# Every third weight piece splits off its low part by an accumulating GpSimd DMA instead of a VectorE subtraction

## The chip, the cores and the metric

The kernel runs on one core of one Trainium2 chip. The time is the device time of one execution in microseconds (us). Two runs of the kernel before took 2231.20 and 2231.25 us; the median shown is 2231.22 us. One further execution was profiled; its rows are the ones quoted below.

## The reference

The reference is a two-layer encoder trunk on 256 tokens of width 2048 in float32. Layer 0 mixes by neighbourhood attention and a gated recurrence, layer 1 by a pooling mixer and grouped-query attention; each mixer sits between a wide input projection and an output projection, and each layer ends in a SwiGLU with 5632 hidden columns:

```python
for layer in range(DEPTH):                      # DEPTH = 2
    y = ab_mixer(x, ...) if layer % 2 == 0 else cd_mixer(x, ...)
    x = layer_norm(DN_ALPHA * x + y, ln_mix_g[layer], ln_mix_b[layer])
    f = (silu(x @ w_gate[layer]) * (x @ w_up[layer])) @ w_down[layer]
    x = layer_norm(DN_ALPHA * x + f, ln_ffn_g[layer], ln_ffn_b[layer])
```

What matters here are the matrix products `x @ w`: all weights are float32 and each is read once.

## The kernel before, in words

**Tiling.** Each weight matrix is cut into 760 pieces of 512 KB: 128 partitions by two blocks of 512 columns. A chunk of output is 512 columns wide for all 256 tokens (two halves of 128, `tok` 0 and 1), accumulated in PSUM (`acc`) over 8 pieces as a rule. TensorE multiplies in the type fp32r, and to keep float32 accuracy both factors are split into a high part (the value rounded to fp32r) and a low part (what is left): `mm3` (L243) issues three matmuls, high by low, high by high and low by high, so a piece costs 2 blocks x 2 token halves x 3 = 12 matmuls.

**A piece's way** (`load_half`, L127 to L148). SyncE issues the load into `raw`, one of 4 buffers (L140). `split` then makes the parts: ScalarE copies `raw` to `whi`, which rounds (L103), and VectorE subtracts, `wlo = raw - whi` (L104). When the subtraction has ended, the `raw` buffer is free for a later load. `whi` and `wlo` lie in a ring of slots (6 from the pool `wp`, 8 in the second mixer, 11 in the out projections and the SwiGLU, since `open_ring` adds 2 and 3), and a slot is free when TensorE has read the piece that lay there. 128 pieces belong to the input projection of layer 0, 40 to that of layer 1, and 592 to the out projections (32 each) and the SwiGLUs (264 each).

**Order.** A scheduler orders the instructions of each engine ahead of time; every engine then runs its own list in order, and SyncE issues its DMAs in order. `tc.high_priority` draws loads and splits forward as far as the buffers allow.

**Norms.** The last chunk before a layer norm is done token half by token half (`tok_major` in `mm_chunk`), with its 8 pieces held. For each half the norm is: statistics and `centre` on VectorE, the power -0.5 of the variance on GpSimd (`rstd`, L200), the scaling on ScalarE (L288), then `flip`: transposes on TensorE (L100), and `xTh` on ScalarE (L317) and `xTl` on VectorE (L319), while GpSimd adds the bias to the residual (`res`, L320), four instructions for a half. The first chunk after the norm is again token-major: it multiplies half 0 while half 1 is still normed. GpSimd also adds the column mask to the attention bias (L635) and fills two tiles per head pair in the mixer of layer 0 (L520, L521). It issues no DMA.

Of the kernel before, what the change touches and what calls it, by code (L numbers as in the profile page):

```python
# [11 lines left out]
F32 = mybir.dt.float32  # L12
F32R = mybir.dt.float32r
I32 = mybir.dt.int32
AF = mybir.ActivationFunctionType
# [57 lines left out]
def trunk(ctx: ExitStack, tc: tile.TileContext, a, out):  # L73
    nc = tc.nc
    mult, add, sub = ALU.mult, ALU.add, ALU.subtract
# [26 lines left out]
    def split(hi, lo, src):  # L102
        nc.scalar.copy(hi, src)  # L103
        nc.vector.tensor_tensor(lo, src, hi.bitcast(F32), op=sub)  # L104
# [16 lines left out]
    last_load = [None]  # L121
    first = [True]

    def load_half(src, between=()):
        behind = ahead if held[0] > 0 else ()
        held[0] -= 1
        slots = [r for r in rings for _ in range(r[1])]  # L127
        pool, bufs = rings[0] if turn[0] < 0 else slots[turn[0] * 3 % len(slots) if len(slots) % 3 else turn[0] % len(slots)]
        turn[0] += 1
        with tc.high_priority(offset=400):  # L130
            raw = wp.tile([P, 2, NCH], F32, tag="raw", name="raw", bufs=4)
            hi = pool.tile([P, 2, NCH], F32R, tag="whi", name="whi", bufs=bufs)
            lo = pool.tile([P, 2, NCH], F32R, tag="wlo", name="wlo", bufs=bufs)
            parts = 1 + len(between)
            n = 2 // parts
            for i in range(parts):
                if i:
                    between[i - 1]()
                s = slice(i * n, (i + 1) * n)
                load = nc.sync.dma_start(raw[:, s, :], src[:, s, :])  # L140
                if first[0]:
                    tc.keep_in_program_order(load)
                last_load[0] = load.ins
                with ExitStack() as order:
                    for ins in behind:
                        order.enter_context(tc.issue_after(ins))
                    split(hi[:, s, :], lo[:, s, :], raw[:, s, :])
        return hi, lo  # L148

    def mm_chunk(halves, lhs, outs, tok_major=False, after=None, before=None):  # L150
# [17 lines left out]
        if tok_major:  # L168
            for i, (src, _) in enumerate(halves):
                if pending and i >= FREE:  # L170
                    held[0] = 1
                loaded.append(load_half(src))
            for tok in range(NT):
                for i in range(n):
                    if pending and i >= FIRST_STEP:
                        step()
                    mms(i, tok, True)
                    if pending and tok == 0:
                        held[0] = HELD
                while pending:  # L180
                    step()
                if after:
                    after(tok)
        else:
            for i, (src, _) in enumerate(halves):
                loaded.append(load_half(src, before(i) if before else ()))
                for tok in range(NT):
                    mms(i, tok)
            if after:
                for tok in range(NT):  # L190
                    after(tok)
# [721 lines left out]
def build(nc, arrays):  # L913
    args = {}
    for name, v in arrays.items():
        t = nc.dram_tensor(name, v.shape, mybir.dt.from_np(v.dtype), kind="ExternalInput")
        args[name[3:]] = t.ap()
    out = nc.dram_tensor("out", (T, D), F32, kind="ExternalOutput").ap()
    with tile.TileContext(nc, schedule_with_timeline_sim=True) as tc:
        trunk(tc, args, out)  # L920
# [11 lines left out]
```

## Time and profile before

| what | value |
|---|---|
| median of the runs | 2231.22 us |
| the profiled execution's own time | 2229.76 us |
| its span, first to last instruction | 2228.0 us |
| mean granted TensorE clock | 0.996 |
| TensorE busy | 2201.6 us (99%) |
| VectorE busy | 1313.6 us (59%) |
| ScalarE busy | 994.5 us (45%) |
| GpSimd busy | 83.1 us (4%) |
| DMA, mean over the span | 189 GB/s |

The profiled execution took 1.76 us more than its span, and 1.46 us less than the median of the runs. Busy times of TensorE are unions of overlapping matmuls. In the rows, PE is TensorE's matmul, PEld its weight load, DVE VectorE, ACT ScalarE, POOL GpSimd, SP SyncE. A row of instructions has start, duration, engine, line, operation, output and inputs; what stands in brackets is the engine's idle time before it and who ended that.

### The profile page before, as it was taken

The numbers are of one execution on the slowest core, as the hardware profiler recorded it, in microseconds if no ns is written. First come the engines' busy times: TensorE is split into PE (matmuls) and PEld (weight loads), VectorE is DVE, ScalarE is ACT, GpSimd is POOL, SyncE is SP. The second block draws the span as 40 slices with busy tenths as digits, with TensorE's granted clock in tenths as the row PEclk, the third lists the DMA queues.
The fourth block names the chain that finished last, engine by engine and source line by source line (L and its number), as shares of the span: only waits on it lengthen the run. The fifth ranks groups of instructions, "written<-read, shape, count | busy, mean of one in ns | idle before, by whom it ended". The sixth has DMA issues, their size and how long they took to land.

```text
span 2228.0 us, 26810 instructions
## 1 busy us (share of the span) xinstructions
PE 2201.6 (99%) x10180; PEld 1833.9 (82%) x10180; DVE 1313.6 (59%) x1662; ACT 994.5 (45%) x1258; POOL 83.1 (4%) x67
## 2 busy tenths in 40 slices
PE   8999999999999999999999999999999999999997
PEld 7888888887888888888888788878888888888886
DVE  6886688667555545554455676665554554544454
ACT  6445544546443444344443564444444444444431
POOL 0010001002000000000000200020000000000001
PEclk9999999999999999999999999999999999999999
DMA  8555545676655556565656464656555555656562
GB/s 293 161 161 180 173 130 183 219 250 211 205 187 191 190 188 194 184 199 184 197 176 199 151 207 141 235 171 227 188 190 192 186 192 186 198 179 201 183 197 71
DMA packets 118898, 420.66 MB, mean 189 GB/s; under 512 B 14448, under 2 KB 17008, under 8 KB 117488
## 3 DMA queue, kind: packets, MB, share of 16 engines
q1 hardware_dynamic: 118768, 418.94, 57.4%
q8 instruction: 80, 1.31, 0.2%
q14 instruction: 50, 0.41, 0.1%
HBM read 416.78 MB, written 2.10 MB: 188 GB/s over the span
## 4 chain that ended last, share of the span: by engine, by line
PE 96%; DVE 2%; ACT 1%; DMA 0%; issue 0%; POOL 0%; DVEq 0%; ACTq 0%; POOLq 0%
PE acc L243 91%; PE tr L100 2%; PE mx L530 1%; PE mx L243 1%; DVE wlo L104 1%; DVE xTl L319 0%; PE mx L576 0%; PE mx L783 0%; ACT whi L103 0%; ACT res L288 0%; DVE res L274 0%; DMA raw<-in_cd_in 0%; DMA x<-in_xT 0%; DVE res L278 0%; PE mx L766 0%
## 5 line engine op out<-in xcount | busy, mean ns | idle before, releaser
L104 DVE TENSOR_TENSOR wlo<-raw,whi 128x1024 fp32r<-128x1024 f32 (+1 forms) x761 | 938.4, 1236 | 726.2 <-ACT whi L103 708.8
L103 ACT CAST whi<-raw 128x1024 fp32r<-128x1024 f32 (+1 forms) x761 | 800.6, 1053 | 987.4 <-PE acc L243 836.2
L243 PE MATMUL acc<-whi,xTl 128*128 128x512 f32 x2080 | 814.7, 394 | 13.7 <-DVE xTl L319 8.0
L243 PE MATMUL acc<-whi,xTh 128*128 128x512 f32 x2080 | 814.4, 392 | 0.0
L243 PE MATMUL acc<-wlo,xTh 128*128 128x512 f32 x2080 | 808.7, 391 | 0.3 <-DVE wlo L104 0.3
L243 PEld LDWEIGHTS acc<-whi,xTl 128*128 128x128 f32 x2080 | 392.3, 189 | 93.5 <-DVE xTl L319 8.5
L243 PEld LDWEIGHTS acc<-wlo,xTh 128*128 128x128 f32 x2080 | 392.0, 188 | 81.6 <-DVE wlo L104 0.7
L243 PEld LDWEIGHTS acc<-whi,xTh 128*128 128x128 f32 x2080 | 392.4, 189 | 78.5
L243 PE MATMUL acc<-whi,yTl 128*128 128x512 f32 x960 | 375.0, 391 | 0.1
L243 PE MATMUL acc<-whi,yTh 128*128 128x512 f32 x960 | 373.8, 389 | 0.0
L243 PE MATMUL acc<-wlo,yTh 128*128 128x512 f32 x960 | 370.0, 389 | 0.0
L243 PEld LDWEIGHTS acc<-wlo,yTh 128*128 128x128 f32 x960 | 180.2, 188 | 37.8 <-DVE wlo L104 0.4
L243 PEld LDWEIGHTS acc<-whi,yTl 128*128 128x128 f32 x960 | 180.3, 188 | 37.0 <-DVE yTl L789 0.3
L243 PEld LDWEIGHTS acc<-whi,yTh 128*128 128x128 f32 x960 | 180.3, 188 | 36.7
L200 POOL TENSOR_TENSOR rstd<-rstd,mhalf 128x4 f32<-128x4 f32 (+2 forms) x18 | 17.6, 976 | 1799.8 <-DVE rstd L197 1656.9
L104 DVE TENSOR_TENSOR yTl<-tr,yTh 128x512 fp32r<-128x512 f32 x48 | 31.1, 686 | 79.5 <-ACT yTh L103 79.5
L103 ACT CAST yTh<-tr 128x512 fp32r<-128x512 f32 x48 | 26.0, 589 | 94.4 <-PE tr L100 94.3
L320 POOL TENSOR_TENSOR res<-res,bet 128x512 f32<-128x512 f32 x24 | 39.4, 1650 | 26.0 <-PE tr L100 14.6
L259 DVE TENSOR_TENSOR res<-res,acc 128x512 f32<-128x512 f32 x32 | 21.9, 685 | 25.4 <-PE acc L243 24.9
L530 PEld LDWEIGHTS mx<-qq,kk 128*128 128x128 f32 x256 | 33.6, 191 | 2.6
L530 PE MATMUL mx<-qq,kk 128*128 128x128 f32 x256 | 33.8, 274 | 0.0
L257 DVE SCALAR_TENSOR_TENSOR res<-res,acc 128x512 f32<-128x512 f32 x32 | 21.8, 683 | 16.7 <-PE acc L243 15.7
(162 smaller groups left out, 829.4 us busy)
## 6 DMA issues: line engine op xcount, KB each, us to landing
raw<-in_gate SPq DMA_DIRECT2D x176, 512.0 KB, 3.9
raw<-in_up SPq DMA_DIRECT2D x176, 512.0 KB, 4.3
raw<-in_down SPq DMA_DIRECT2D x176, 512.0 KB, 4.1
raw<-in_ab_in SPq DMA_DIRECT2D x127, 512.0 KB, 4.1
raw<-in_cd_in SPq DMA_DIRECT2D x40, 512.0 KB, 4.3
raw<-in_ab_out SPq DMA_DIRECT2D x32, 512.0 KB, 4.7
raw<-in_cd_out SPq DMA_DIRECT2D x32, 512.0 KB, 4.0
x<-in_xT SPq DMA_DIRECT2D x8, 256.0 KB, 6.3
```

The costliest lines, as they stand in the source:

```text
L100: return nc.tensor.transpose(o, src, eye)
L103: nc.scalar.copy(hi, src)
L104: nc.vector.tensor_tensor(lo, src, hi.bitcast(F32), op=sub)
L200: nc.gpsimd.tensor_tensor(r[:, :n], r[:, :n], mhalf[:, :n], op=ALU.pow)
L243: ins = nc.tensor.matmul(o, lhs[a], rhs[b], start=start and n == 0, stop=stop and n == 2)
L257: nc.vector.scalar_tensor_tensor(r, r, ALPHA, psum, op0=mult, op1=add)
L259: nc.vector.tensor_tensor(r, r, psum, op=add)
L320: nc.gpsimd.tensor_tensor(r, r, bet[:, s], op=add)
L530: nc.tensor.matmul(m[:, 2 * h + s, :], kk[:, h, s * P : (s + 1) * P], qq[:, h, r * P : (r + 1) * P], start=True, stop=True,)
```

## The change

Of the 760 pieces every third one (those with a `between`, the first, apart) is split by `split_by_dma`: 253 pieces. ScalarE copies `raw` to `whi` as before, then writes `wlo = -whi` with a second instruction, and a DMA issued on GpSimd's queue adds `raw` to `wlo` in SBUF. The sum is left as a float32 word and isn't rounded to fp32r. VectorE does nothing for these pieces. The diff:

```diff
@@ -121,7 +121,17 @@
     last_load = [None]
     first = [True]
 
+
+    pieces_in = [0]
+
+    def split_by_dma(hi, lo, raw):
+        nc.scalar.copy(hi, raw)
+        nc.scalar.activation(lo, hi.bitcast(F32), AF.Copy, scale=-1.0)
+        nc.gpsimd.dma_start(lo.bitcast(F32), raw, accum_op=add)
+
     def load_half(src, between=()):
+        pieces_in[0] += 1
+        by_dma = pieces_in[0] % 3 == 0 and not between
         behind = ahead if held[0] > 0 else ()
         held[0] -= 1
         slots = [r for r in rings for _ in range(r[1])]
@@ -144,7 +154,7 @@
                 with ExitStack() as order:
                     for ins in behind:
                         order.enter_context(tc.issue_after(ins))
-                    split(hi[:, s, :], lo[:, s, :], raw[:, s, :])
+                    (split_by_dma if by_dma else split)(hi[:, s, :], lo[:, s, :], raw[:, s, :])
         return hi, lo
```

In the changed kernel all lines behind the insertion stand 10 further down: L140 becomes L150, L320 becomes L330, and so on; the copy, the negation and the DMA of a third piece have the lines L128, L129 and L130. The lists of the engines move with it, at two places that the prediction speaks of.

The first is SyncE's list in the first down projection of layer 0. In brackets is what an instruction waits for: a name with DMAHW is a load, DVE is VectorE, a name with DMASW one of eight semaphores that the adds of GpSimd's queue use in turn. Before:

```order
L140 DMA raw_5558<-in_down0 128x1024 [waits DMAHW4_49,DVE_49]
L140 DMA raw_5576<-in_down0 128x1024 [waits DMAHW5_49,DVE_49]
L140 DMA raw_5594<-in_down0 128x1024 [waits DMAHW6_49,DVE_49]
L140 DMA raw_5616<-in_down0 128x1024 [waits DMAHW7_49,DVE_49]
L140 DMA raw_5634<-in_down0 128x1024 [waits DMAHW0_49,DVE_49]
L140 DMA raw_5652<-in_down0 128x1024 [waits DMAHW1_49,DVE_49]
```

Every load waited for a subtraction. Now the same place reads (raw_5591, raw_5646 and raw_5705 are third pieces):

```order
L150 DMA raw_5610<-in_down0 128x1024 [waits DMAHW4_49,DVE_49]
L150 DMA raw_5628<-in_down0 128x1024 [waits DMAHW3_49,DMASW4_49]
L150 DMA raw_5646<-in_down0 128x1024 [waits DMAHW5_49,DVE_49]
L150 DMA raw_5665<-in_down0 128x1024 [waits DMAHW7_49,DVE_49]
L150 DMA raw_5687<-in_down0 128x1024 [waits DMAHW6_49,DMASW5_49]
L150 DMA raw_5705<-in_down0 128x1024 [waits DMAHW0_49,DVE_49]
L150 DMA raw_5724<-in_down0 128x1024 [waits DMAHW2_49,DVE_49]
L150 DMA raw_5742<-in_down0 128x1024 [waits DMAHW1_49,DMASW6_49]
```

One load in three now waits for an add, and it is that of the third piece five pieces earlier: raw_5687 waits for the add of raw_5591, with raw_5610, raw_5628, raw_5646 and raw_5665 between. The load right behind the waiting one is a third piece's own.

The second place is GpSimd's list at the norm between the out projection and the SwiGLU of layer 0. Before (res0 and res1 are the residuals of token halves 0 and 1):

```order
L200 TENSOR_TENSOR rstd_4366<-rstd_4366,mhalf_70 128x1 [waits DVE_49]
L320 TENSOR_TENSOR res0_3792<-res0_3792,bet_3803 128x512 [waits DMAHW2_49,DMAHW5_49,PE_49,Activation_49]
L320 TENSOR_TENSOR res0_3792<-res0_3792,bet_3803 128x512 [waits PE_49,Activation_49] x3
L200 TENSOR_TENSOR rstd_4485<-rstd_4485,mhalf_70 128x1 [waits DVE_49]
L320 TENSOR_TENSOR res1_3793<-res1_3793,bet_3803 128x512 [waits DMAHW3_49,PE_49,Activation_49]
L320 TENSOR_TENSOR res1_3793<-res1_3793,bet_3803 128x512 [waits PE_49,Activation_49] x3
```

Now (wlo_4567, wlo_4586 and wlo_4605 belong to pieces 2, 5 and 8 of the first gate chunk, wlo_4808 to the up chunk behind it):

```order
L130 DMA wlo_4567<-raw_4565 128x1024 [waits DMASW5_49,DMAHW3_49,DVE_49,Activation_49]
L210 TENSOR_TENSOR rstd_4419<-rstd_4419,mhalf_70 128x1 [waits DVE_49]
L130 DMA wlo_4586<-raw_4584 128x1024 [waits DMAHW6_49,DMASW6_49,Activation_49]
L330 TENSOR_TENSOR res0_3834<-res0_3834,bet_3845 128x512 [waits PE_49] x2
L330 TENSOR_TENSOR res0_3834<-res0_3834,bet_3845 128x512 [waits PE_49,Activation_49] x2
L210 TENSOR_TENSOR rstd_4538<-rstd_4538,mhalf_70 128x1 [waits DVE_49]
L330 TENSOR_TENSOR res1_3835<-res1_3835,bet_3845 128x512 [waits PE_49,Activation_49] x3
L130 DMA wlo_4605<-raw_4603 128x1024 [waits DMAHW1_49,DMASW7_49,Activation_49]
L130 DMA wlo_4808<-raw_4806 128x1024 [waits DMAHW4_49,DMASW0_49,Activation_49]
L330 TENSOR_TENSOR res1_3835<-res1_3835,bet_3845 128x512 [waits PE_49]
```

The add of the last piece of the gate chunk stands behind three of the four residual additions of half 1. At the two other norms that a token-major chunk follows, the list has the same pattern: the add of that chunk's eighth piece behind three additions to the residual of half 1.

## The prediction

> **What bounds the kernel now.** I read the page first, then the stretches by stage, the chain of waits in one of them, and the waits.
>
> ```profile
> span 2228.0 us, 26810 instructions
> PE 2201.6 (99%) x10180; PEld 1833.9 (82%) x10180; DVE 1313.6 (59%) x1662; ACT 994.5 (45%) x1258; POOL 83.1 (4%) x67
> q1 hardware_dynamic: 118768, 418.94, 57.4%
> ...
> PE 96%; DVE 2%; ACT 1%; DMA 0%; issue 0%; POOL 0%; DVEq 0%; ACTq 0%; POOLq 0%
> ```
>
> TensorE is busy for all but 26.4 us of the span, and 96% of the chain that ended last is its own work. VectorE, which the change relieves, is 2% of that chain. The stretches say where the 26.4 us lie (columns: stretch, its length, busy us of PE, PEld, DVE, ACT, POOL with counts, clock, DMA share, GB/s):
>
> ```profile
> 0.00:60.00 60.00, 54.34 (x235) 44.43 (x236) 38.19 (x52) 36.51 (x47) 1.67 (x9) 1.00 0.80 281
> 60.00:440.00 380.00, 380.00 (x1956) 323.27 (x1955) 287.04 (x530) 180.54 (x274) 24.80 (x18) 1.00 0.55 169
> 520.00:1160.00 640.00, 636.00 (x2846) 527.11 (x2845) 332.27 (x309) 274.74 (x294) 6.49 (x4) 1.00 0.59 195
> 1500.00:2140.00 640.00, 640.00 (x2865) 530.71 (x2864) 326.61 (x298) 271.09 (x278) 0.00 (x0) 1.00 0.59 193
> ```
>
> In the SwiGLUs and in the first mixer TensorE never waits; it does so only at the start, at the norms and at the end. The chain in a SwiGLU gives the pace:
>
> ```profile
> 1581.97 43.57 PE acc L243 x192
> 1625.54 0.88 PE tr L100 x8
> 1626.41 13.62 PE acc L243 x60
> ```
>
> 192 matmuls, 16 pieces, take 1626.41 - 1581.97 = 44.44 us with the transposes: 2.78 us per piece. And the waits show who waits for whom in steady work:
>
> ```profile
> ACT whi L103 <- PE acc L243: 836.2, 590, 11.2
> ...
> PE acc L243 <- DVE wlo L104: 0.3, 1, 0.3
> ```
> ```profile
> SPq L140 <- DVE wlo L104: 1587.2, 684, 13.1
> ```
>
> ScalarE's copies wait for slots that TensorE has not left yet, so the split parts lie ready far ahead; TensorE waits 0.3 us in all directly for a low part. SyncE waits for subtractions, since these free the `raw` buffers. There is little to win: even with no idle moment the matmuls need 2201.6 us of span, 1.2% less.
>
> **The change part by part.** The split's own instructions:
>
> ```profile
> L104 DVE TENSOR_TENSOR wlo<-raw,whi 128x1024 fp32r<-128x1024 f32 x759 | 937.0, 1238 | 725.8 <-ACT whi L103 708.5 <-PE acc L243 0.4
> L103 ACT CAST whi<-raw 128x1024 fp32r<-128x1024 f32 x759 | 799.3, 1054 | 987.0 <-PE acc L243 836.2 <-issue 65.8 <-DMA raw<-in_ab_out 17.7
> ```
>
> *Removed*: 253 x 1.238 = 313 us of VectorE. They lie beside TensorE's work nearly everywhere, so I count nothing for them; the gain is a rival. *Added on ScalarE*: 253 negations of the copy's size, 253 x 1.054 = 267 us; ScalarE comes to 1261 us, 57%, and its idle time in front of the copies alone is 987 us, so this is hidden while a slot is the last to come. *Added on GpSimd*: 253 adds. The trace has no DMA from GpSimd and none with arithmetic, so I bound one add, from its issue to its landing, by the nearest rows (L140 between 1500 and 2140 us; a store from SBUF; POOL's shortest and longest groups):
>
> ```profile
> DMA to landing us min/median/max: 3.3/4.2/6.1
> ```
> ```profile
> out<-res SPq DMA_DIRECT2D x8, 256.0 KB, 2.3
> ```
> ```profile
> L200 POOL TENSOR_TENSOR rstd<-rstd,mhalf 128x4 f32<-128x4 f32 (+2 forms) x18 | 17.6, 976 | 1799.8 <-DVE rstd L197 1656.9
> L635 POOL TENSOR_TENSOR bias<-bias,colmask 128x512 f32<-128x512 f32 x8 | 17.6, 2206 | 97.2 <-ACT pth L103 55.3 <-DMA bias<-in_na_bias 39.2 <-ACT whi L103 2.7
> ```
>
> A piece occupies the DMA engines for 57.4% x 2228 us / 418.94 MB x 0.524 MB = 1.6 us. From below, the add is the 2.3 us of a store of half the size plus half a piece: 3.1 us. From above it is the slowest load, 6.1 us, two further passes over the data, 3.2 us, and 2.2 us of GpSimd: 11.5 us. I take a load's median of 4.2 us, since the add moves a load's bytes under the same traffic, plus one pass for reading the low part too, 1.6 us, plus 1.0 us for GpSimd to issue it: **6.8 us**.
>
> [...]
>
> *The wait that this moves* is that of SyncE. In the list of the changed kernel the load five pieces behind a third piece waits for its add, and the load behind that one is a third piece's own. So from one third piece to the next but one, six pieces or 6 x 2.78 = 16.7 us, there follow each other: the add, a load's landing 4.2 us, the next load 1.6 us behind it, copy 1.05, negation 1.05, and the next add. The add may last 16.7 - 7.9 = **8.8 us** before the ring of `raw` buffers turns slower than TensorE. At 6.8 us it fits with 2 us to spare, and the 11 slots keep ten pieces of lead. Steady stages: 0.
>
> *The norms* have no such cover. At the first one:
>
> ```profile
> 519.23 1.29 POOL L320 TENSOR_TENSOR res<-res,bet 128x512 f32<-128x512 f32 x1 [3.18 <-ACT res L288]
> 521.05 6.11 POOL L320 TENSOR_TENSOR res<-res,bet 128x512 f32<-128x512 f32 x3 [0.53 <-PE mx L100]
> ...
> 523.04 0.40 PE L243 MATMUL acc<-wlo,xTh 128*128 128x512 f32 x1
> ...
> 528.57 0.50 PE L243 MATMUL acc<-whi,xTl 128*128 128x512 f32 x1 [4.00 <-DVE xTl L319]
> ```
>
> The add of the gate chunk's eighth piece stands behind the third addition, which ended at 521.05 + 2 x 6.11 / 3 = 525.1. Its landing is then at 531.9, where TensorE wanted this low part at 523.04. Behind it come four matmuls (0.9 us) and four transposes (0.44 us), so half 1 begins at 533.3 instead of 528.57: 4.7 us. The other two norms have the same pattern:
>
> ```profile
> 1261.77 1.71 POOL L320 TENSOR_TENSOR res<-res,bet 128x512 f32<-128x512 f32 x1 [0.53 <-PE tr L100]
> ...
> 1264.01 6.15 PE acc L243 x27
> ```
> ```profile
> 1489.24 6.12 POOL L320 TENSOR_TENSOR res<-res,bet 128x512 f32<-128x512 f32 x3 [0.53 <-PE mx L100]
> ...
> 1496.76 3.35 PE acc L243 x7
> ```
>
> 1263.5 + 6.8 + 1.3 = 1271.6 against 1264.0 is 7.6 us; 1493.3 + 6.8 + 1.3 = 1501.4 against 1496.8 is 4.6 us. Together 16.9 us.
>
> *The start* has no lead either. Piece 3 is copied here, and its first low part is wanted here:
>
> ```profile
> 11.71 1.05 ACT L103 CAST whi<-raw 128x1024 fp32r<-128x1024 f32 x1 [0.63 <-DMA raw<-in_ab_in]
> ...
> 14.44 0.39 PE L243 MATMUL acc<-wlo,xTh 128*128 128x512 f32 x1
> ```
>
> Copy and negation end at 13.8, the add lands at 20.6: 6.2 us late.
>
> *The mixers*: with 6 slots a third piece is needed five pieces after its slot came free, 13.9 us later, and is ready after 1.05 + 1.05 + 6.8 = 8.9 us: 5.0 us to spare. An add that stands behind a waiting GpSimd instruction can lose that:
>
> ```profile
> 345.43 1.29 POOL L635 TENSOR_TENSOR bias<-bias,colmask 128x512 f32<-128x512 f32 x1 [20.83 <-DMA bias<-in_na_bias]
> 350.03 7.21 POOL L635 TENSOR_TENSOR bias<-bias,colmask 128x512 f32<-128x512 f32 x1 [3.31 <-DMA bias<-in_na_bias]
> ```
>
> Most waits of this kind end within the spare; the first of these can hold an add for some 10 us, 5 more than there are. I count one: 5 us; none would be 0, all of them is a rival.
>
> **The sum.** On the profiled execution's 2229.76 us: 0 + 16.9 + 6.2 + 5 = 28.1, so 2257.9; the median of the runs lies 1.46 us higher: **2259 us**, 1.2% slower, which is within the 2% that a measurement of this kernel can tell from no change. With an add of 3.1 us the norms cost 5.8, the start 2.5 and the mixers nothing: 2240. This forecast ends where the add passes 8.8 us, with about 2276.
>
> **The rivals.** *The raw ring turns slower than TensorE.* For it: the spare is 2 us in a quantity that I have only by analogy, and loads and adds stretch each other on engines that are 59% busy. Against it: slots ten pieces deep, which smooth single delays. At 10 us per add each six pieces take 1.2 us more; 592 pieces make 592 / 6 x 1.2 = 118, and norms and start 4 x 3.2 = 13 on top: 2390. It decides from 8.8 us on, and passes 2% some 0.1 us later. *The DMA engines are the bound*: if reading, reading and writing pass one after the other, an add takes 4.8 us of them, and three pieces 4.8 + 4.8 = 9.6 instead of 8.33. Over 592 / 3 thirds that is 250 us: 2510. The point is 3.5 us per add. For it speaks that no row shows the arithmetic; against it that a load's 1.6 us holds a read and a write already. *GpSimd's list holds adds in the mixers*: ten waits there, each 3.5 us past the spare, give 35: 2294; for it the 20.83 us row, against it that most such waits in the trace begin long before anything is due. *A gain*: at the norms subtractions are in TensorE's way:
>
> ```profile
> 521.55 6.70 DVE wlo L104 x3
> ...
> 1474.04 3.45 DVE wlo L104 x2
> ...
> 1491.95 4.50 DVE wlo L104 x2
> ```
>
> If these 14.6 us vanished and the add took 3.1 us, the time would be 2231 + 8.4 - 14.6 = 2225. Against it: only one piece in three is relieved.
>
> **How the numbers follow.** Forecast 0.44 (its own range 2238 to 2276), raw ring 0.26 (to 2430), DMA engines 0.16 (to 2700), GpSimd's list 0.08, gain 0.06. Slower by over 2% are the ring, the engines and the list: 0.50. Within 2%: 0.44 and nearly all of the gain, 0.49. Faster by over 2%, under 2187, would need more than the 26.4 us of idle: 0.01. The range leaves out the gain's part below 2236 and the engine case beyond 2500.
>
> **What would show it.** Right: L130 issues on GpSimd land in 6 to 8 us, TensorE stays full between 1500 and 2140 us, and new waits of PE for DMA into `wlo` appear at 14, 523, 1263 and 1490 us. Wrong: in that stretch PE waits for `wlo` regularly and its busy share falls, with SyncE waiting for the adds (raw ring: DMA share under 0.9; engines: near 1); or the waits of PE sum up between 60 and 440 us behind L635, L520 or L200 (GpSimd's list).

## The result, and the profile after

| | before | after |
|---|---|---|
| median of the runs, us | 2231.22 (2 runs) | 2378.35 (2 runs, 2376.8 to 2379.9) |
| profiled execution, us | 2229.76 | 2376.8 |
| its span, us | 2228.0 | 2375.0 |
| mean granted clock of TensorE | 0.996 | 0.977 |

The ratio is 1.0659, 95% interval 1.0614 to 1.0705: the change makes the kernel 147 us slower. The forecast was 2259 us. The figure nearest to the measured one is that of the first rival, the ring of `raw` buffers, 2390 us.

The matmuls, L243 before, are L253 in the changed kernel. The page of the changed kernel, in the same parts as that of before (the last rows are DMA issues: instructions, KB each, median us from issue to landing):

```profile
span 2375.0 us, 27620 instructions
...
PE 2250.5 (95%) x10180; PEld 1854.9 (78%) x10180; DVE 1000.3 (42%) x1409; ACT 1239.8 (52%) x1511; POOL 296.2 (12%) x320
...
q1 hardware_dynamic: 118768, 418.94, 52.9%
q0 software_dynamic: 36432, 132.66, 29.2%
...
DMA 57%; PE 24%; issue 11%; ACT 4%; DVE 2%; SPq 1%; POOL 0%; POOLq 0%; ACTq 0%; DVEq 0%
...
wlo<-raw POOLq DMA_DIRECT2D x253, 512.0 KB, 7.0
raw<-in_gate SPq DMA_DIRECT2D x176, 512.0 KB, 5.4
```

The chain that ended last was 96% TensorE's; now 57% of it is time in which a DMA is under way. The loss divides in two. TensorE's idle time went from 26.4 to 2375.0 - 2250.5 = 124.5 us, 98 more. And the same 10180 matmuls are busy for 2250.5 us where it was 2201.6, 49 more, at a lower granted clock. The stretches (columns as before: length, busy us of PE, PEld, DVE, ACT, POOL, clock, DMA share, GB/s) say where:

```profile
60.00:440.00 380.00, 378.11 (x1942) 320.60 (x1941) 242.33 (x490) 218.61 (x317) 54.15 (x56) 1.00 0.78 222
560.00:1220.00 660.00, 634.52 (x2774) 520.27 (x2773) 218.54 (x211) 334.45 (x346) 66.80 (x76) 0.98 0.86 239
1600.00:2260.00 660.00, 633.33 (x2778) 520.58 (x2777) 219.55 (x211) 335.40 (x347) 66.31 (x76) 0.98 0.86 239
```

The first mixer is nearly full, as forecast. In the SwiGLUs TensorE now idles 26 us in 660, and the DMA engines are at 0.86, under 0.9: of the marks set down for the raw ring these two have come. So has the third, that SyncE waits for the adds:

```profile
SPq L150 <- DMA wlo<-raw: 1056.4, 245, 9.1
SPq L150 <- DVE wlo L104: 616.0, 257, 8.2
```
```profile
ACT whi L103 <- DMA raw<-in_down: 153.4, 80, 6.0
ACT whi L103 <- PE acc L253: 144.4, 96, 5.7
...
ACT whi L128 <- PE acc L253: 84.7, 69, 5.1
```

SyncE's loads wait for 245 of the 253 adds, since these hold the `raw` buffers. ScalarE's copies, which waited 836 us for slots that TensorE had yet to leave, wait 144 us for them and those of the third pieces 85, and otherwise for loads: the slots are no longer full.

The last mark, that TensorE waits for `wlo` regularly, has not come in the SwiGLUs. Between 560 and 1220 us its waits, 25.4 us, all end with the instructions that empty its accumulators: L384, L267 and L269 on VectorE, L377 on ScalarE. The largest part of them, and VectorE just before the longest one (TensorE's idle time there is 4.32 us, and its next instruction starts at 863.62):

```profile
PE tr L100 <- DVE sil L384: 11.0, 3, 4.3
```
```profile
861.75 1.23 DVE L104 TENSOR_TENSOR wlo<-raw,whi 128x1024 fp32r<-128x1024 f32 x1 [3.68 <-ACT whi L103]
862.89 1.28 DVE L384 TENSOR_TENSOR sil<-sil,acc 128x512 f32<-128x512 f32 x2
```

In VectorE's list the product L384 stands behind the subtraction of a piece that was drawn forward. This subtraction waits for ScalarE's copy, and that one stood behind the copy and negation of a third piece whose load landed only at 858.5. So late loads reach TensorE through the order of the lists. The four other waits of over 3 us in this stretch (up to 646.66, 732.90, 1003.43 and 1142.57) have a subtraction with a late copy just before them in the same way.

The chain inside the first SwiGLU shows the ring turning (start, length, what):

```profile
838.60 9.57 DMA wlo<-raw
...
849.11 9.43 DMA raw<-in_up
...
858.61 2.56 issue
...
861.18 4.76 DMA wlo<-raw
...
866.38 4.38 DMA raw<-in_up
...
870.82 3.93 issue
...
874.77 10.31 DMA wlo<-raw
```

An add lands; a load that waited for its buffer goes out, and right behind it a third piece's own load, which is the one shown; that piece is copied and negated (the stretch called issue); its add goes out. No matmul stands in this chain. Two turns, each from a third piece to the next but one, take 874.77 - 838.60 = 36.2 us, 18.1 each, where six pieces take TensorE 16.7. The load's leg is 9.43 in the first turn, where two other loads and an add had gone out within 1 us ahead of it, and 4.38 in the second, where one load had. The times to landing (us, min/median/max), first of the adds and then of the loads, between 560 and 1220 us:

```profile
DMA to landing us min/median/max: 4.4/8.2/10.8
```
```profile
DMA to landing us min/median/max: 3.3/5.2/10.2
```

By stage, counted from the start of the multiplication that makes `rstd` of the second token half at each of the four norms (the small GpSimd instruction on 128x1), in us and with the difference from before:

| kernel | start to norm 1 | norm 1 to 2 (SwiGLU 0) | norm 2 to 3 (mixer, out projection) | norm 3 to 4 (SwiGLU 1) |
|---|---|---|---|---|
| before | 515.05 | 740.47 | 227.80 | 735.46 |
| after | +26.2 | +47.2 | +24.7 | +49.0 |
| swiglu_only | +2.2 | +50.7 | 0.0 | +42.6 |
| swiglu_only_raw6 | +2.0 | -1.7 | 0.0 | -2.6 |
| outside_only | +26.6 | +3.6 | +27.4 | +5.7 |
| mixers_only | +12.0 | 0.0 | +10.7 | 0.0 |
| norms_only | +2.0 | +3.5 | +13.1 | +3.9 |
| out_proj_only | +6.2 | +0.3 | +2.3 | +0.2 |

The first stage of kernels that begin alike spreads by some 2 us. So of 147 us the two stages of the SwiGLUs lost 96, and the rest of the program 51. The late adds behind norms 1 and 3 fall into the stages of the SwiGLUs. The kernels in the lower rows are experiments, told below.

### The profile page after: what moved, and what is told of

Read it like the earlier page. It is cut to its first block, busy times and chain, and to the rows that moved or that the text cites. A ratio compares the mean times of both kernels' runs of the same rounds, so it can differ in the third digit from the quotient of the medians.

```text
span 2375.0 us, 27620 instructions
## 1 busy us (share of the span) xinstructions
PE 2250.5 (95%) x10180; PEld 1854.9 (78%) x10180; DVE 1000.3 (42%) x1409; ACT 1239.8 (52%) x1511; POOL 296.2 (12%) x320
## 3 DMA queue, kind: packets, MB, share of 16 engines
q1 hardware_dynamic: 118768, 418.94, 52.9%
q0 software_dynamic: 36432, 132.66, 29.2%
## 4 chain that ended last, share of the span: by engine, by line
DMA 57%; PE 24%; issue 11%; ACT 4%; DVE 2%; SPq 1%; POOL 0%; POOLq 0%; ACTq 0%; DVEq 0%
DMA wlo<-raw 28%; PE acc L253 20%; DMA raw<-in_down 10%; DMA raw<-in_gate 8%; DMA raw<-in_up 7%; DMA raw<-in_ab_in 2%; DMA raw<-in_cd_in 1%; ACT whi L103 1%; SPq L150 1%; PE mx L540 1%; DVE wlo L104 1%; DMA raw<-in_ab_out 1%; PE mx L253 1%; PE tr L100 1%; ACT whi L128 1%
## 5 line engine op out<-in xcount | busy, mean ns | idle before, releaser
L104 DVE TENSOR_TENSOR wlo<-raw,whi 128x1024 fp32r<-128x1024 f32 (+1 forms) x508 | 623.4, 1232 | 1180.8 <-ACT whi L103 1143.0
L103 ACT CAST whi<-raw 128x1024 fp32r<-128x1024 f32 (+1 forms) x508 | 529.4, 1046 | 660.9 <-DMA raw<-in_down 153.4
L253 PE MATMUL acc<-wlo,xTh 128*128 128x512 f32 x2080 | 817.8, 395 | 35.3 <-DMA wlo<-raw 34.7
L253 PE MATMUL acc<-whi,xTl 128*128 128x512 f32 x2080 | 824.3, 397 | 18.4 <-ACT sil L377 7.7
L253 PE MATMUL acc<-whi,xTh 128*128 128x512 f32 x2080 | 820.5, 394 | 0.0
L253 PEld LDWEIGHTS acc<-wlo,xTh 128*128 128x128 f32 x2080 | 395.8, 190 | 121.3 <-DMA wlo<-raw 38.5
L253 PEld LDWEIGHTS acc<-whi,xTl 128*128 128x128 f32 x2080 | 396.4, 191 | 104.2 <-ACT sil L377 12.0
L253 PEld LDWEIGHTS acc<-whi,xTh 128*128 128x128 f32 x2080 | 396.2, 190 | 79.8
L130 POOL DMA_DIRECT2D wlo<-raw x253 | 221.4, 875 | 1890.8 <-ACT wlo L129 1722.0
L128 ACT CAST whi<-raw 128x1024 fp32r<-128x1024 f32 x253 | 266.1, 1052 | 340.4 <-PE acc L253 84.7
L253 PE MATMUL acc<-whi,yTl 128*128 128x512 f32 x960 | 382.4, 398 | 24.9 <-DVE res L269 13.1
L253 PE MATMUL acc<-wlo,yTh 128*128 128x512 f32 x960 | 376.4, 397 | 10.6 <-DMA wlo<-raw 10.6
L253 PE MATMUL acc<-whi,yTh 128*128 128x512 f32 x960 | 379.2, 395 | 0.0
L129 ACT ACTIVATE wlo<-whi 128x1024 fp32r<-128x1024 f32 x253 | 268.4, 1061 | 7.0
L253 PEld LDWEIGHTS acc<-whi,yTl 128*128 128x128 f32 x960 | 183.9, 192 | 67.0 <-DVE res L269 15.9
L253 PEld LDWEIGHTS acc<-wlo,yTh 128*128 128x128 f32 x960 | 183.4, 191 | 51.7 <-DMA wlo<-raw 12.4
L253 PEld LDWEIGHTS acc<-whi,yTh 128*128 128x128 f32 x960 | 183.7, 191 | 37.8
L100 PE MATMUL tr<-ident,sil 128*128 128x128 f32 x176 | 28.6, 300 | 22.8 <-DVE sil L384 22.8
L100 PEld LDWEIGHTS tr<-ident,sil 128*128 128x128 f32 x176 | 22.9, 153 | 29.8 <-DVE sil L384 26.7
L104 DVE TENSOR_TENSOR yTl<-tr,yTh 128x512 fp32r<-128x512 f32 x48 | 31.4, 685 | 25.4 <-ACT yTh L103 25.0
L330 POOL TENSOR_TENSOR res<-res,bet 128x512 f32<-128x512 f32 x24 | 37.0, 1575 | 31.2 <-PE mx L100 19.2
```

Of the source, the lines that this page charges most:

```text
L100: return nc.tensor.transpose(o, src, eye)
L128: nc.scalar.copy(hi, raw)
L129: nc.scalar.activation(lo, hi.bitcast(F32), AF.Copy, scale=-1.0)
L130: nc.gpsimd.dma_start(lo.bitcast(F32), raw, accum_op=add)
L253: ins = nc.tensor.matmul(o, lhs[a], rhs[b], start=start and n == 0, stop=stop and n == 2)
L330: nc.gpsimd.tensor_tensor(r, r, bet[:, s], op=add)
```

## The experiments

Theory 1 is the raw ring: an add holds a `raw` buffer so long that the four buffers turn slower than TensorE. Theory 2 is that the DMA engines have too much work. Theory 3 is that ScalarE's negations and the order of the engines' lists cost the time. Every ratio is to the kernel before on the same chip, with its 95% interval.

**Ring, engines or lists: four kernels.** *raw6*: two more `raw` buffers in the memory of the out projections and SwiGLUs, the split as in the change.

```diff
-            raw = wp.tile([P, 2, NCH], F32, tag="raw", name="raw", bufs=4)
+            k = raws_in[0] % (4 + more[1])
+            raws_in[0] += 1
+            if k < 4:
+                raw = wp.tile([P, 2, NCH], F32, tag="raw", name="raw", bufs=4)
+            else:
+                raw = more[0].tile([P, 2, NCH], F32, tag="raw", name="raw", bufs=more[1])
...
+        more[:] = [fp, 2]
         xT = out_proj(...)
```

> The changed kernel with six instead of four raw buffers in the out projections and the SwiGLUs; every load there then reuses the buffer of six pieces earlier. Theory 1, the raw ring: an add of 8 us holds a buffer too long for four buffers, so with six the pace returns to 2.78 us per piece there, the DMA share staying near 0.86 to 0.9, and only norms, start and mixers cost: 2265 to 2295 us. Theory 2, the DMA engines: three loads and an add fill them so unevenly that the pace is theirs, whatever the buffers: 2350 to 2380 us. Theory 3, the lists: the second ScalarE instruction and the reordered lists cost the time: 2360 to 2380 us.

*bystander*: the kernel before, and in the out projections and SwiGLUs an adding DMA of the high part of each third piece into scratch memory, whose sum nothing reads.

```diff
                     split(hi[:, s, :], lo[:, s, :], raw[:, s, :])
+                    if scrap and pieces_in[0] % 3 == 0:
+                        nc.gpsimd.dma_start(scrap[pieces_in[0] % 2], hi.bitcast(F32), accum_op=add)
```

> The kernel before, with an accumulating GpSimd DMA of 512 KB for every third piece of the out projections and SwiGLUs that adds the piece's high part to a scratch tile that nothing reads: 197 adds with the engines' full load, but none frees a raw buffer and TensorE waits for none. Theory 1: the engines have room, loads land later but in time: 2231 to 2245 us. Theory 2: the loads starve as in the changed kernel: 2320 to 2360 us. Theory 3 has no say here beyond 2231, since VectorE still splits.

*vector_add*: copy and negation stay on ScalarE, VectorE does the add.

```diff
-        nc.gpsimd.dma_start(lo.bitcast(F32), raw, accum_op=add)
+        nc.vector.tensor_tensor(lo, raw, lo.bitcast(F32), op=add)
```

> The changed kernel with the add of the third pieces on VectorE in place of the DMA (copy and negation on ScalarE, then low part plus raw words on VectorE). Theories 1 and 2: without the DMA the loss is gone, 2228 to 2240 us. Theory 3: the negation on ScalarE and the list around it cost most of the 147 us, so 2300 us or more.

*plain_copy*: the DMA writes the raw words over the low part; the subtraction of those pieces is left out.

```diff
-        nc.gpsimd.dma_start(lo.bitcast(F32), raw, accum_op=add)
+        nc.gpsimd.dma_start(lo.bitcast(F32), raw)
```

> The changed kernel with the GpSimd DMA copying the raw words over the negated high part instead of adding them (the addition is left out, so the low parts of the third pieces are other numbers). Issue, wait and landing stay, and only the second read of the add goes: by half the packet time, 0.16 instead of 0.33 us per 4 KB, a DMA should land some 1.5 to 3 us earlier, at 5 to 6 us. Theory 1: that brings six pieces of the ring to 16.7 us or less, 2255 to 2290 us. Theory 2: the engine time of three pieces falls from 7.4 to 6.2 us, so 2255 to 2290 us as well; the two part here only by whether loads still land late. Theory 3: 2360 to 2380 us.

| kernel | median us | ratio |
|---|---|---|
| raw6 | 2316.8 | 1.0383 [1.0368, 1.0399] |
| bystander | 2251.0 | 1.0086 [1.0069, 1.0103] |
| vector_add | 2232.5 | 1.0002 [0.9993, 1.0011] |
| plain_copy | 2261.1 | 1.0130 [1.0115, 1.0145] |

Theory 3 loses the negations with vector_add: 253 of them, and 253 additions on VectorE in place of the subtractions, cost nothing and gain nothing. The order of the lists with a DMA in them is plain_copy's question, below. Theory 2 loses its strongest form with bystander. Its stretch in the first SwiGLU, and the landing of its own adds there:

```profile
560.00:1160.00 600.00, 599.31 (x2684) 496.44 (x2683) 307.43 (x278) 254.60 (x262) 64.05 (x74) 1.00 0.90 258
```
```profile
scrap<-whi POOLq DMA_DIRECT2D x198, 512.0 KB, 7.2
raw<-in_gate SPq DMA_DIRECT2D x176, 512.0 KB, 6.2
```

The engines carry more than in the changed kernel, 0.90 against 0.86, with as many adds, and TensorE is full. What was taken away is that a `raw` buffer and a low part wait for an add, and the negations, which vector_add acquits. The page also gives the prices at TensorE's own pace: an add 7.2 us, a load 5.8 to 6.2 by weight matrix, where the loads of before took 4.2. Bystander's loss of 19 us, 6 more than the expectation allowed, lies in the stages with the out projections (14.8 and 9.9 us; the stages of the SwiGLUs changed by -4.75 and 0.15); its cause there was not followed.

raw6 is half a success, 22 us above the expected range. In the SwiGLUs its loss is gone (norm 1 to 2: 742.0 us, +1.6; norm 3 to 4: 739.1, +3.7). But the stages with the out projections lost 41.5 and 45.7 us, more than in the change. A wait of SyncE's queue tells why:

```profile
SPq L157 <- DVE yTl L806: 34.3, 1, 34.3
```

The changed kernel has no such wait: the two new buffers lie in memory that the second mixer still used, and the queue goes in order, so one load held up all behind it for 34 us. It is a mishap of this kernel, and swiglu_only_raw6 below is free of it. Why the first of the two stages lost more than in the change is not shown.

plain_copy has as many DMAs of the same size behind the same instructions, and in the stages of the SwiGLUs it loses 0.6 and 2.4 us; so the order of the lists does not by itself cost the 96 us either. Its 29 us lie in the two other stages (11.7 and 17.3). Its DMAs land in 4.3 us at the median, and hold the engines for less:

```profile
q0 software_dynamic: 36432, 132.66, 14.4%
...
wlo<-raw POOLq DMA_DIRECT2D x253, 512.0 KB, 4.3
```

14.4% of a span of 2260.0 us over 253 is 1.29 us of the engines for a copy; in the changed kernel 29.2% of 2375.0 over 253 is 2.74 us for an add. So the arithmetic doubles the transfer, and it is the add's length that the ring does not bear.

**Threshold or price per add, and where: four kernels.** A further theory 4 says that each add costs the same, 147 / 253 = 0.58 us, wherever it stands. A condition chooses the pieces; `part` holds the stage and whether the chunk is token-major:

```diff
-        by_dma = pieces_in[0] % 3 == 0 and not between
+        by_dma = pieces_in[0] % 3 == 0 and not between and (part[0] == "ffn" and not part[1])
```

*swiglu_only* has this line.

> Pieces are split by the DMA add only in the SwiGLUs, without the two token-major chunks of each (about 165 adds of 253); four raw buffers as in the change. Theory 1 (the raw ring, a threshold): the two SwiGLUs lost 47 and about 48 us in the changed kernel, and they lose it here again: 2232 + 95 = 2327. Theory 4 (each add costs the same wherever it stands, 147 / 253 = 0.58 us): 2232 + 165 x 0.58 = 2328. This run alone does not tell the two apart; the next three do.

*swiglu_only_raw6* has it too, and two more buffers, used from the first piece of a SwiGLU on:

```diff
+            k = raws_in[0] % 6 if more[0] else 0
...
+        more[0] = fp
         xT = ffn(fp, 0, xT, res, load_gb(fp, 0, "ffn"), False)
```

> The same pieces as in swiglu_only, and two more raw buffers, taken from the SwiGLU's own memory and used only once the SwiGLU has begun. Theory 1: the ring has room, TensorE is full, 2230 to 2237. Theory 4: as many adds, so 2328 as without the buffers.

*outside_only* has the opposite condition, `part[0] != "ffn" or part[1]`.

> The complement of swiglu_only: the add only in the mixers, the out projections and the token-major chunks at the norms (about 88 adds); four raw buffers. Theory 1: what is left of the loss, 147 - 95 = 52 us: 2284, nearly all of it before the first norm (26) and between the second and the third (25). Theory 4: 2232 + 88 x 0.58 = 2283. If the sum of this loss and of swiglu_only's is far under 147, the parts feed each other.

*sixth_piece*: `pieces_in[0] % 6 == 0` in place of `% 3`, everywhere.

> The add for every sixth piece instead of every third, everywhere (126 adds); four raw buffers. Theory 1: one add in a turn of 12 pieces, 33 us, in which the chain of add, load, load, copy and negation of 16 to 25 us fits with room: the SwiGLUs lose nothing, and what remains is half of the norms and the out projections: 2232 + 10 to 30 = 2242 to 2262. Theory 4: half of the loss, 2232 + 73 = 2305.

| kernel | median us | ratio |
|---|---|---|
| swiglu_only | 2307.6 (2292.4 to 2325.2) | 1.0317 [1.0268, 1.0365] |
| swiglu_only_raw6 | 2225.9 | 0.9971 [0.9960, 0.9982] |
| outside_only | 2293.2 | 1.0277 [1.0261, 1.0293] |
| sixth_piece | 2258.0 | 1.0119 [1.0103, 1.0135] |

Theory 4 falls twice: half as many adds cost 26 us and not 73, and 164 adds in the SwiGLUs cost 76 us with four buffers and less than nothing with six. The losses of swiglu_only and outside_only, 76 and 61, make 137 of 147, so the stages stand nearly for themselves. The expectations had been 2327 and 2284; swiglu_only's executions spread by 33 us, and its profiled one is the slowest of them, 2325.2. The first SwiGLU of swiglu_only_raw6:

```profile
560.00:1160.00 600.00, 600.00 (x2688) 497.56 (x2688) 215.03 (x204) 324.52 (x332) 63.97 (x74) 1.00 0.89 257
```

The time lies below the expected 2230 to 2237 us. TensorE is full, with a third of the low parts coming by DMA and the DMA engines busier than in the changed kernel.

**The ring without an add, and the control.** *raw6_alone* is swiglu_only_raw6 with the condition `False`: no add, six buffers in the SwiGLUs.

> The kernel before with no add at all, and the two further raw buffers of swiglu_only_raw6 in the SwiGLUs: the control for its 0.9971. If the buffers alone made that gain: 2226, ratio 0.997. If the add made it, because VectorE has fewer subtractions where the norms end (TensorE's idle time there went from 4.0 to 1.8 us at two norms): 2231, ratio 1.000. By the profile of before, in which copies wait for slots and not for raw buffers, I expect 1.000.

*raw2_swiglu* has no add either, and in the SwiGLUs two buffers in place of four.

```diff
-            raw = wp.tile([P, 2, NCH], F32, tag="raw", name="raw", bufs=4)
+            if not more[0]:
+                raw = wp.tile([P, 2, NCH], F32, tag="raw", name="raw", bufs=4)
+            else:
+                raw = more[0].tile([P, 2, NCH], F32, tag="raw", name="raw", bufs=2)
```

> The kernel before with no add, and in the SwiGLUs two raw buffers instead of four: the ring law without any add. Theory 1: two pieces take a load's landing of 4.2 us, the copy 1.05 and the subtraction 1.24, some 6.6 us with the hops between them, where TensorE takes 2 x 2.78 = 5.56; 528 pieces in the SwiGLUs are 264 pairs, 264 x 1.04 = 275 us: about 2507, more where the granted clock falls to half behind TensorE's idle gaps as in the changed kernel (it would show that the gaps do that, not the adds). If a ring of buffers does not set the pace: 2232.

raw6_alone: 2231.75 us, ratio 1.0000 [0.9991, 1.0009]. Buffers alone bring nothing. raw2_swiglu: 2339.4 us, ratio 1.0485 [1.0466, 1.0505], so a ring that is too short sets the pace with no add in the program. Its chain in the first SwiGLU, and its busy times:

```profile
839.73 3.40 DMA raw<-in_up
...
843.23 1.06 ACT whi L103
...
844.31 1.24 DVE wlo L104
...
845.57 3.44 DMA raw<-in_up
```
```profile
PE 2235.5 (96%) x10180; PEld 1837.8 (79%) x10180; DVE 1301.9 (56%) x1662; ACT 987.9 (42%) x1258; POOL 76.6 (3%) x67
```

One turn is 845.57 - 839.73 = 5.84 us for two pieces, which take TensorE 5.56. If all turns are like this one, the 264 pairs of the SwiGLUs lose 264 x 0.28 = 74 us by it, and the same matmuls are busy 2235.5 - 2201.6 = 34 us longer; together 108 us, where the loss is 107. I had expected 275 us, because I put in the landing of 4.2 us of the full kernel; here, with two buffers in place of four, a load lands in 3.4 at the median. Over the loads of the SwiGLUs the landing took 3.4 us here, 3.9 to 4.3 before and 5.8 to 6.2 beside bystander's adds, at 178, 191 and 258 GB/s in the first SwiGLU, so it followed the traffic in this direction too.

**Outside the SwiGLUs: three kernels**, by the condition alone: `part[1]` (norms_only), `part[0] == "out_proj" and not part[1]` (out_proj_only), `part[0] == "mixer" and not part[1]` (mixers_only).

> The add only for the pieces of the token-major chunks, which stand around the norms (some 20 adds); four raw buffers. The prediction's own term for the norms was 16.9 us: 2249. If the ring in the out projections and mixers made most of the 61 us of outside_only, this is much less: outside_only lost 3.5 us between the first norm and the second, and 5.7 behind the third, where only such chunks have adds; about 10 us for three norms, 2242.

> The add only for the third pieces of the first three chunks of the two out projections (16 adds); four raw buffers. In outside_only the loads of the out projections waited for adds and TensorE for both. If the ring alone makes the loss there, both out projections lose 10 to 15 us each: 2252 to 2262. If they lose only because the mixer ahead of them has used up the lead, they begin here with the lead of before and lose little: 2232 to 2240; then the mixers' own adds are what outside_only pays for.

> The add only for pieces of the two mixers, the first three of the program among them, without the token-major chunks; four raw buffers. outside_only lost 61 us, norms_only 20 and out_proj_only 8. If the parts simply add, the mixers and the start lose 33 us: 2265. If the parts feed each other (a mixer hands the out projection a shorter lead), the mixers alone lose the 5 us of TensorE's idle time and some 4 of half clock at the start, and a few more: 2240 to 2250. The prediction's own terms were 6.2 for the start and 5 for the mixers: 2243.

| kernel | median us | ratio |
|---|---|---|
| norms_only | 2252.1 | 1.0095 [1.0081, 1.0109] |
| out_proj_only | 2239.5 | 1.0043 [1.0030, 1.0056] |
| mixers_only | 2251.7 | 1.0090 [1.0073, 1.0107] |

They lose 20, 8 and 21 us, 49 together, and outside_only, which has all three, 61. So some 13 us come only when the parts stand together; that one part uses up the lead of the next is likely, but no run shows it. Plain adding would have left 33 us for the mixers, and they cost 21. Two waits that the forecast had placed are here, the first of norms_only, the second of mixers_only (start, length, instruction, idle time ahead of it and what ended it):

```profile
533.77 0.80 PE L255 MATMUL acc<-wlo,xTh 128*128 128x512 f32 x1 [8.74 <-DMA wlo<-raw]
```
```profile
20.42 0.80 PE L255 MATMUL acc<-wlo,xTh 128*128 128x512 f32 x1 [4.34 <-DMA wlo<-raw]
```

**Are the engines a second bound close behind?** *half_raw7*: swiglu_only_raw6 with `% 2` in place of `% 3`, and seven buffers.

> swiglu_only_raw6 with every second piece of the SwiGLUs by the add instead of every third, and seven raw buffers there instead of six. Engines: by the shares of the changed kernel's page an add holds the DMA engines 29.2% x 2375 / 253 = 2.74 us and a load 52.9% x 2375 / 799 MB-pieces of 0.524 = 1.57 us; two loads and an add are 5.88 us where two pieces take TensorE 5.56, so if the engines set the pace here the some 248 pairs lose 0.32 us each, 79 us: 2305, with the DMA share near 1. If the ring alone counts, seven buffers give 19.5 us for a chain of add, load, copy and negation of 16 to 19: 2226 to 2240.

2229.5 us, ratio 0.9993 [0.9984, 1.0002]. Its page, and its second SwiGLU:

```profile
q1 hardware_dynamic: 118768, 418.94, 53.7%
q0 software_dynamic: 35712, 130.04, 30.1%
...
wlo<-raw POOLq DMA_DIRECT2D x248, 512.0 KB, 8.6
...
raw<-in_down SPq DMA_DIRECT2D x176, 512.0 KB, 7.4
```
```profile
1540.00:2140.00 600.00, 600.00 (x2688) 497.09 (x2687) 172.69 (x166) 360.77 (x368) 94.50 (x109) 1.00 1.02 289
```

By these shares two loads and an add are 2 x 53.7% x 2225.4 / 799 + 30.1% x 2225.4 / 248 = 5.69 us of the engines where TensorE takes 5.56, and the share is shown as 1.02. Still TensorE has not one idle moment in 600 us. The share therefore overstates the work a little, and what the engines can do lies at or beyond this point; the 79 us of the expectation did not come. And the adds land later here than in the first SwiGLU of the change, 8.6 us against 8.2, the loads 7.4 against 5.2, for no loss at all, since seven buffers cover it. This is the plainest sign that it is not the length of a transfer that costs, but its length against the turn of the ring.

## Why the prediction was wrong, step by step

**The step that failed** is "The add may last 16.7 - 7.9 = 8.8 us before the ring of `raw` buffers turns slower than TensorE. At 6.8 us it fits with 2 us to spare ... Steady stages: 0." The chain in it is the right one; the trace goes round it in that order. Its prices were those of a program without the adds. The landing of 4.2 us belongs to engines that are 59% busy; the adds themselves bring these to 0.9, and bystander shows what they then take while TensorE keeps its pace: an add 7.2 us, a load 5.9 (the median in its second SwiGLU; 6.0 in the first). With the next load 1.6 and copy and negation 2.1 the turn is 7.2 + 5.9 + 1.6 + 2.1 = 16.8 us of 16.7. The spare of 2 us was none. The two turns of the changed kernel that are shown above were longer still. On average the add took 7.2 us (6.8 in the forecast), the third piece's load went out 0.7 behind the add's landing (1.6) and landed after 6.9 (4.2), and 3.3 passed up to the next add (2.1), since ScalarE had other copies in between: 18.1 us for 14.7. So the add was nearly right, and the term most under-sized is the load's landing. I had named the effect against myself ("loads and adds stretch each other on engines that are 59% busy") and put it into a rival's chance, when its size could have been put into the sum. Over the whole first SwiGLU adds landed in 8.2 us and loads in 5.2 at the median. The stages of the SwiGLUs lost 96 us; 9 of them had been forecast, for norms 1 and 3, and the other 87 stood at 0.

**The lead of ten pieces** did not smooth this, as the forecast hoped, and it was not used up either. Up to 858 us 1061 matmuls that read a low part had started, four to a piece, so 265 pieces; 182 pieces had been subtracted and 90 adds issued by then, 272 together. (Before, it was 282 and 291.) TensorE stood idle with some seven pieces split ahead of it, for the reason shown above: the instructions that empty its accumulators stand in the lists of VectorE and ScalarE behind the split of pieces drawn far forward. A lead helps only what waits for the pieces themselves, and the forecast had no term for the lists. No run changed this order alone.

With six buffers the load that waits for an add is at least six pieces behind it, so that no second load stands in the turn: 7.2 + 5.9 + 2.1 = 15.2 us of 16.7 by the same prices. That 1.5 us of spare was enough.

**The rival's figure**, 2390 us, was worked out from a 10 us add and the unloaded load. The measured 2378 is near, but by other terms: adds of 8.2 us with loads of 5.2, and a third of the loss by a lower clock, for which it had no term. That the figure fits is in part luck. At an add of 8.8 us, where the forecast was to end, its own sum gives 2259 + 4 x 2.0 = 2267 us and not 2276.

**The norms**: 16.9 us forecast, 20 measured alone. The first one's late low part was forecast to land at 531.9; TensorE took it up at 533.77, in an execution that ran 2 us behind up to there. By stage the three cost 3.5, 13.1 and 3.9 against 4.7, 7.6 and 4.6. The second is under-sized: I had followed one add there, and TensorE waited for two, the second time for 6.12 us:

```profile
1263.73 0.50 PE L255 MATMUL acc<-wlo,xTh 128*128 128x512 f32 x1 [0.96 <-DMA wlo<-raw]
...
1278.85 0.79 PE L255 MATMUL acc<-wlo,xTh 128*128 128x512 f32 x1 [6.12 <-DMA wlo<-raw]
```

**The start**: the landing was forecast for 20.6 us, and TensorE began at 20.42. The delay is right; it cost more than itself, since the matmuls behind it went at half pace, one every 0.43 us in place of 0.23, up to 26.1 us. **The mixers**: 5 us forecast for both; mixers_only lost 12.0 and 10.7 in the two stages, start included.

**The clock** is missing from the forecast altogether. 49 of the 147 us are the same matmuls busy for longer; the mean granted clock gives nearly the same, (1 - 0.977) x 2375 - (1 - 0.996) x 2228 = 46 us. Each late add was priced by its delay alone (the rows are in the last section).

**The rival of the DMA engines** is refuted for this kernel: full TensorE at a share of 0.90 with as many adds (bystander), and at 1.02 (half_raw7). It needed 4.8 us of the engines for an add; by the shares on the changed kernel's page an add took 2.74 and a load 52.9% x 2375 / 799 = 1.57, so three loads and an add take 7.5 of the 8.33 us. **GpSimd's list** was to show between 60 and 440 us; there TensorE idles 1.9 us in all. In the second mixer of mixers_only TensorE has these two waits:

```profile
PE acc L255 <- DMA wlo<-raw: 3.5, 2, 3.2
...
PE acc L255 <- DVE rstd L211: 3.2, 1, 3.2
```

The second one ends with VectorE, whose own waits for this `rstd` in the stretch from 1270 to 1500 us are for ScalarE (4.8 us in all, the longest 2.3), and not with GpSimd.

**The gain** is real, and was hidden. With room in the ring and no add near a norm, swiglu_only_raw6 is 0.9971 of before, some 6 us, and raw6_alone shows that the buffers have no part in it. Its stretches around the first and third norm:

```profile
500.00:540.00 40.00, 38.20 (x177) 31.29 (x176) 31.50 (x57) 28.92 (x56) 16.93 (x12) 0.96 0.54 169
1470.00:1510.00 40.00, 38.19 (x185) 31.46 (x184) 31.51 (x55) 31.35 (x58) 16.94 (x12) 1.00 0.64 192
```

TensorE idles 1.8 us in each where raw6_alone has 36.0 of 40 busy, 4.0 idle; its waits for the normalised input fall from 8.0 to 3.6 us. That VectorE has fewer subtractions ahead of it is the likely reason. That accounts for 4.4 us, and the stages agree with -1.7 and -2.6; what lies beyond that, within some 2 us of scatter, is not settled. half_raw7 idles the same 1.8 us at these norms, and waits 3.8 us for the product `sil` some 40 us behind them; whether this is why its median keeps less of the gain, no run shows. Of the two kernels and all variants, swiglu_only_raw6 is the fastest, 2225.9 us.

What stays open besides: the 13 us by which the parts outside the SwiGLUs cost more together than apart were not divided further, and the bound of the DMA engines was not reached.

## What to carry to other kernels

A transfer that takes the place of an engine's instruction, as the add did here, holds its source buffer from the issue to the landing (7.0 us at the median, and the next load into the buffer waited for 245 of the 253 adds), and the ring of buffers has to turn within the consumer's time; work out that turn with the latencies that hold once the new traffic is there, not with those of the profile before, and take the slowest seen ones if there is no spare to catch up. Before giving up the idea add a buffer: here, where the DMA share in the first SwiGLU grew from 0.59 to 0.85 (swiglu_only), two buffers turned a loss of 76 us into a gain of 6. Do not count on a deep lead before you have looked which other instructions stand behind the prefetched work in an engine's list; here TensorE waited 4.32 us with some seven pieces split ahead of it. And keep such a transfer out of the places that have no lead, the start (a wait of 4.34 us here) and the stretch behind a norm (8.74).

## What the runs showed of the hardware that was not expected

**Idle time costs more than itself.** In raw2_swiglu, which has no adding DMA, TensorE's matmuls around an idle moment (start, length):

```profile
611.12 0.39 PE L260 MATMUL acc<-whi,xTh 128*128 128x512 f32 x1
615.08 1.11 PE L100 MATMUL tr<-ident,sil 128*128 128x128 f32 x4 [3.57 <-DVE sil L393]
615.84 0.77 PE L260 MATMUL acc<-whi,xTl 128*128 128x512 f32 x1
...
620.48 0.57 PE L260 MATMUL acc<-wlo,xTh 128*128 128x512 f32 x1
620.88 0.40 PE L260 MATMUL acc<-whi,xTl 128*128 128x512 f32 x1
```
```profile
642.88 0.50 PE L260 MATMUL acc<-whi,xTl 128*128 128x512 f32 x1 [1.39 <-ACT sil L386]
643.21 0.39 PE L260 MATMUL acc<-whi,xTh 128*128 128x512 f32 x1
```

After 3.57 us without work the matmuls follow one another about every 0.43 us in place of 0.23, until 620.9, some 5.8 us after the restart, and the granted clock from 610 to 620 us is 0.70; after 1.39 us they do not, and from 640 to 650 us it is 1.00. This kernel has no adds, so the fall of the clock came with idle time and not with the adds. How much idle time it takes is not settled: in raw2_swiglu no slow matmuls follow an idle time of 2.90 us (at 840.36; the clock is 1.00 from 830 to 850 us), while in the changed kernel some follow one of 1.95 us (at 769.40), at a granted clock of 0.50 from 771 to 774 us. In the waits followed here the pace came back some 3 us (863.62 to 866.6 us in the changed kernel) to 5.8 us after the restart. In the changed kernel the slower matmuls are a third of the loss, 49 of 147 us.

**An adding DMA costs twice a copying one**: 2.74 us of the engines for 512 KB against 1.29, and 7.0 us to landing against 4.3, both issued by GpSimd and within on-chip memory.

**A DMA share over 1**: half_raw7's 1.02 with a full TensorE shows that a share near 1 does not yet prove that the engines set the pace.
